# Seven block products for twelve of the pairs in one feed-forward up projection of a two-layer diffusion backbone

## The chip, the core and the metric

The kernel runs on one core of a Trainium2 chip. The metric is the device time of one execution in microseconds (us). Below, TensorE (PE in the rows; PEld is its weight load), VectorE (DVE), ScalarE (ACT), GpSimd (POOL) and the queue of SyncE (SP), which issues nearly all fetches, are the core's engines. SBUF is the core's memory, PSUM the eight banks that TensorE writes to.

## What is computed

Two layers; each is a feed-forward block, a token mixer and a second feed-forward block. There are 256 context tokens and 256 latent tokens of 1024 features; in layer 2, context tokens are only needed until the mixer has read them. The part that matters here:

```python
def modulate(h, shift, scale):
    return h * (1.0 + scale) + shift

def swiglu(u, w_up, w_down):
    a, v = jnp.split(u @ w_up, 2, axis=-1)
    return (jax.nn.silu(a) * v) @ w_down

def ffn_sublayer(h, m, j, w_up, w_down, g, b):
    u = modulate(h, m[:, :, 3 * j], m[:, :, 3 * j + 1])
    return post_norm(h, swiglu(u, w_up, w_down), m[:, :, 3 * j + 2], FFN_RES_W, g, b)
```

The modulation vectors `m` (nine for each layer) are `silu(c) @ w_ada + b_ada`, once for the latent tokens and once for the context. The hidden width is 2816, 22 tiles of 128: a gate tile and a value tile for each, here called a pair.

## The kernel before, in words

All data is kept with features on the partitions, so a block of tokens is 128 features x 512 tokens (`T`; 256 context, then 256 latent, `TL`). Every operand of a large matmul is split into a high and a low part, both in a 32-bit format for TensorE, and a product is three passes: high x high, high x low, low x high (`mm3`, L369 to L375, passes L372 to L374). The low part is the value less the high part.

Weights come in groups: one fetch of 512 KB brings eight blocks of 128x128 in one of three raw buffers (`raw_issue`, L255; tiles `wr`). ScalarE copies the group into its high part (L342, tile `wh`), VectorE subtracts to get the low part (L344, tile `wl`), and the raw buffer goes to the next fetch on SP's queue, in a fixed order (`split_ahead`). Three slots hold split groups; in a down product three more are taken from the activations, which are free by then. A slot is free when TensorE has read its group.

The feed-forward function (`ffn`) begins with the first two pairs, whose matmuls follow the layer norm feature by feature (`k_outer`). Then come the other pairs one by one: eight blocks of the contraction for the gate, eight for the value, 48 matmuls in two banks. `act` applies the SiLU on ScalarE (L760), the product on VectorE (L761) and the split of the hidden tile (L764, L765). Then come the eight row tiles of the down product, 22 blocks each; the last two are done in halves of 256 tokens (`tail`), with all their split weights held for the second half, so in the first half a group is used up in the time of 24 matmuls of 256 columns.

The modulation vectors are made by VectorE on the side: one tile (`ada_part`, L481) is a fetch of 512 KB into a raw buffer of the same three and, for each of the two conditioning vectors, a multiplication with a sum over 1024 elements (L488), then a bias (L492). 128 tiles are spread in program order over the feed-forward blocks: one in each of the up projections' contractions, two in each row of a down product.

The program is written once without a chip, which gives the order of the weight groups, and again to emit. A scheduler sets the order on each engine.

```python
                    if kt == KT // 2:
                        self.ada_part()
...
                if ft in (8, 16):
                    self.ada_part()
```

## Time and profile before

| what | value |
|---|---|
| median of three runs | 2718.85 us (2718.21 to 2720.57) |
| the profiled execution, its own time | 2722.64 us |
| its span, from first to last instruction | 2720.7 us |
| mean granted TensorE clock | 0.991 |
| busy share of the span | PE 98%, DVE 71%, ACT 45%, POOL 13% |
| fetched from memory | 373.63 MB, 139 GB/s over the span |

The profile is of one execution. Busy matmuls overlap in it, since the end of each is modelled: what a matmul costs in a stream is the distance from its start to the next one's start. In a row of the timeline, square brackets give the idle time of the engine before the instruction and what ended it.

The feed-forward stages in this execution: layer 1 first block, pairs to 265 us, down product after it; layer 1 second block, pairs to 1452, down product to 1577; layer 2 first block (the one that is changed), pairs 1604 to 1822, down product to 1945; layer 2 second block (latent tokens alone, so 256 columns), pairs 2511 to 2642.

### The profile page before, as it was taken

The numbers are of one execution on the slowest core, as the hardware profiler recorded it, in microseconds if no ns is written. First come the engines' busy times: TensorE is split into PE (matmuls) and PEld (weight loads), VectorE is DVE, ScalarE is ACT, GpSimd is POOL, SyncE is SP. The second block draws the span as 40 slices with busy tenths as digits, with TensorE's granted clock in tenths as the row PEclk, the third lists the DMA queues.
The fourth block names the chain that finished last, engine by engine and source line by source line (L and its number), as shares of the span: only waits on it lengthen the run. The fifth ranks groups of instructions, "written<-read, shape, count | busy, mean of one in ns | idle before, by whom it ended". The sixth has DMA issues, their size and how long they took to land.

```text
span 2720.7 us, 38673 instructions
## 1 busy us (share of the span) xinstructions
PE 2659.9 (98%) x14869; PEld 2280.2 (84%) x14869; DVE 1928.3 (71%) x3469; ACT 1222.9 (45%) x1755; POOL 353.8 (13%) x296
## 2 busy tenths in 40 slices
PE   9999999999999999999999999999998999999998
PEld 7888897778887888888888888888977898899997
DVE  5788769599877545468887588633697998676654
ACT  4323237963345344433323142332388745574543
POOL 0000132112121000040000130001312112012002
PEclk9999999999999999999999999999999999999999
DMA  7666534134343222235666446532333354343563
GB/s 280 193 189 200 172 122 130 60 99 149 105 134 109 78 86 78 88 99 170 194 195 191 132 129 199 169 120 97 108 123 105 111 174 150 107 142 124 175 191 116
DMA packets 117833, 380.49 MB, mean 140 GB/s; under 512 B 13888, under 2 KB 22352, under 8 KB 117648
## 3 DMA queue, kind: packets, MB, share of 16 engines
q1 hardware_dynamic: 116000, 373.52, 42.5%
q0 software_dynamic: 1504, 4.34, 0.5%
q8 instruction: 116, 1.90, 0.3%
q14 instruction: 69, 0.57, 0.1%
q10 hardware_dynamic: 144, 0.17, 0.0%
HBM read 373.63 MB, written 4.33 MB: 139 GB/s over the span
## 4 chain that ended last, share of the span: by engine, by line
PE 56%; DVE 7%; ACT 3%; issue 2%; DMA 1%; POOL 0%; SPq 0%; POOLq 0%; DVEq 0%; ACTq 0%
PE bank L372 17%; PE bank L373 17%; PE bank L374 17%; PE bank L1282 1%; PE bank L1262 1%; DVE wl L344 1%; DVE x L869 1%; DMA wr<-in_ws_dram 1%; DMA x<-acs_d 1%; DVE f L669 0%; DVE m1l L344 0%; ACT wh L342 0%; PE bank L921 0%; DVE f L670 0%; DVE f L676 0%
## 5 line engine op out<-in xcount | busy, mean ns | idle before, releaser
L342 ACT ACTIVATE wh<-wr 128x1024 fp32r<-128x1024 f32 x388 | 410.2, 1058 | 727.1 <-PE bank L373 493.2
L344 DVE TENSOR_TENSOR wl<-wr,wh 128x1024 fp32r<-128x1024 f32 x388 | 483.6, 1247 | 239.4 <-ACT wh L342 237.6
L488 DVE SCALAR_TENSOR_TENSOR ada_scr<-wr,sb 128x1024 f32<-128x1024 f32 x256 | 316.7, 1237 | 135.9 <-DMA wr<-in_ws_dram 133.2
L372 PE MATMUL bank<-u0h,wh 128*128 128x512 f32 (+1 forms) x660 | 247.1, 376 | 5.5 <-ACT u0h L675 3.8
L372 PE MATMUL bank<-r,wh 128*128 128x512 f32 (+1 forms) x736 | 251.3, 342 | 0.0
L374 PE MATMUL bank<-r,wl 128*128 128x512 f32 (+1 forms) x736 | 249.9, 340 | 0.0
L373 PE MATMUL bank<-r,wh 128*128 128x512 f32 (+1 forms) x736 | 249.7, 340 | 0.0
L374 PE MATMUL bank<-u0h,wl 128*128 128x512 f32 (+1 forms) x660 | 237.2, 360 | 3.9 <-DVE wl L344 3.9
L373 PE MATMUL bank<-u0l,wh 128*128 128x512 f32 (+1 forms) x660 | 236.2, 358 | 2.1 <-DVE u0l L677 2.0
L373 PE MATMUL bank<-u1l,wh 128*128 128x512 f32 (+1 forms) x660 | 235.1, 357 | 0.8 <-DVE u1l L677 0.7
L372 PE MATMUL bank<-u1h,wh 128*128 128x512 f32 (+1 forms) x660 | 233.5, 356 | 0.6 <-ACT u1h L675 0.6
L374 PE MATMUL bank<-u1h,wl 128*128 128x512 f32 (+1 forms) x660 | 234.0, 355 | 0.0
L372 PE MATMUL bank<-u2h,wh 128*128 128x512 f32 (+1 forms) x660 | 233.6, 355 | 0.0
L374 PE MATMUL bank<-u2h,wl 128*128 128x512 f32 (+1 forms) x660 | 233.4, 354 | 0.0
L373 PE MATMUL bank<-u2l,wh 128*128 128x512 f32 (+1 forms) x660 | 233.2, 354 | 0.0
L373 PE MATMUL bank<-u3l,wh 128*128 128x512 f32 (+1 forms) x644 | 228.6, 355 | 1.5 <-DVE u3l L677 1.5
L372 PE MATMUL bank<-u3h,wh 128*128 128x512 f32 (+1 forms) x644 | 228.3, 356 | 0.0
L374 PE MATMUL bank<-u3h,wl 128*128 128x512 f32 (+1 forms) x644 | 228.0, 354 | 0.0
L372 PEld LDWEIGHTS bank<-r,wh 128*128 128x128 f32 x736 | 139.4, 190 | 15.3 <-issue 0.3
L374 PEld LDWEIGHTS bank<-r,wl 128*128 128x128 f32 x736 | 139.5, 190 | 15.1
L373 PEld LDWEIGHTS bank<-r,wh 128*128 128x128 f32 x736 | 139.5, 190 | 14.8
L372 PEld LDWEIGHTS bank<-u0h,wh 128*128 128x128 f32 x660 | 125.6, 191 | 29.7 <-issue 5.6
(530 smaller groups left out, 5919.4 us busy)
## 6 DMA issues: line engine op xcount, KB each, us to landing
wr<-in_ws_dram SPq DMA_DIRECT2D x602, 512.0 KB, 4.0
m1r<-in_ws_dram SPq DMA_DIRECT2D x29, 512.0 KB, 3.9
ada<-in_ws_dram SPq DMA_DIRECT2D x16, 512.0 KB, 9.0
x<-acs_d SPq DMA_DIRECT2D x22, 256.0 KB, 3.4
x<-acs_d SPq DMA_DIRECT2D x39, 128.0 KB, 3.6
x<-in_lw_dram SPq DMA_DIRECT2D x16, 256.0 KB, 3.2
f<-acs_d SPq DMA_DIRECT2D x25, 128.0 KB, 3.4
sb<-s_d SPq DMA_DIRECT2D x6, 512.0 KB, 5.8
```

Source lines behind the costliest of these rows:

```text
L342: self.pin(nc.scalar.activation(hi, raw, AF.Copy))
L344: self.pin(nc.vector.tensor_tensor(lo, raw, hi, op=ALU.subtract))
L372: x = self.pin(nc.tensor.matmul(out, st[0], mv[0], start=start, stop=False, skip_group_check=True))
L373: self.pin(nc.tensor.matmul(out, st[0], mv[1], start=False, stop=False, skip_group_check=True))
L374: self.last_mm = self.pin(nc.tensor.matmul(out, st[1], mv[0], start=False, stop=stop, skip_group_check=True))
L488: nc.vector.scalar_tensor_tensor(self.ada_scr, raw.rearrange("p a b -> p (a b)"), 1.0, self.sb[b], op0=ALU.mult, op1=ALU.mult, accum_out=o ...
L869: nc.vector.scalar_tensor_tensor(ys[:, :, a:z], xs[:, :, a + o:z + o], w(k), ys[:, :, a:z], op0=ALU.mult, op1=ALU.add)
L1262: nc.tensor.matmul(ps[:, 0:256], cc(kt[d], a), vv(a), start=True, stop=True)
L1282: nc.tensor.matmul(cc(po[w], c), lh, rh, start=n == 0, stop=n == len(steps) - 1, skip_group_check=True)
```

## The change

It concerns layer 2's first feed-forward block (`paired`), and the place of the modulation tiles in the others.

Of the 22 pairs there, the first four stay as they were. The other 18 go through `strassen`. Of every three, two are block products and the third is done as before, in four parts. In a block product the weights of a pair are a 2x2 block matrix (gate and value by even and odd blocks of the contraction), the activations are one too (even and odd blocks by context and latent tokens), and the four blocks of the result come from seven products (Winograd's form) of 4 blocks x 3 passes with 256 columns, where eight such products did it before. The sums of weights (four of 128x512 a pair) and of results (three of 128x256) are on VectorE; ScalarE copies what a bank holds between two products that add to the same bank (left half: products 1, 6, 5, 3; the other bank: 7, 4 and 2). Every operand of a product is split by itself, 512 columns at a time, into half a slot (`Part`), so the three slots hold the operands of six products. `products` gives their order.

The differences of the activations are made once, after the layer norm (`columns`): it writes the modulated activations as 32-bit values to a new tile (`ucol`), four subtractions and four splits of 128x1024 follow. For room, that stage has only 8 hidden tiles in split form, the other 14 are kept as they are and split while the first row of the down product runs (`late_parts`, two for each block), the low parts into the activations' place; after that row they are copied out of it on ScalarE (`move`), and the three extra slots of that down product come after it. There are two more raw buffers for the stage.

The modulation tiles leave the stage. A tile is now also taken after 12 blocks of a row in layer 1's first down product, and after 4 and 12 in its second one; what is left goes to layer 2's last up projection. By the order of the built programs the 128 tiles lie so: layer 1 first block 50 before and 56 now, layer 1 second block 52 and 64, layer 2 first block 26 and none, layer 2 second block none and 8.

```diff
+KSPLIT = (0, 2, 4, 6, 1, 3, 5, 7)
+NFULL = 8
+def products(n):
+    r, rest = [], []
+    for p in range(n):
+        last = p == n - 1
+        if p % 3 == 2:
+            r += [(p, 11)] + rest + [(p, 12), (p, 21), (p, 22)]
+            rest = []
+        else:
+            r += [(p, 1), (p, 7)] + rest + [(p, m) for m in ((6, 4, 5, 2) if last else (6, 4, 2, 5))]
+            rest = [(p, 3)]
+    return r + rest
...
+            if m in (1, 7, 11, 21):
+                n = i + 2 * p + (m in (7, 21))
+                R[p, 1 if m in (1, 11) else 7] = self.raw_next(tuple(self.wlist[8 * n:8 * n + 8])), len(self.seq) - 1
+            g = R[p, 1][0]
+            a11, a12 = flat(g[:, 0:4]), flat(g[:, 4:8])
+            if m not in (1, 11, 12):
+                v = R[p, 7][0]
+                a21, a22 = flat(v[:, 0:4]), flat(v[:, 4:8])
+            if m in (1, 11):
+                src = a11
+            elif m == 21:
+                src = a21
+            elif m == 7:
+                R[p, 5] = self.F()
+                sub(R[p, 5], a21, a22, ALU.add)
+                sub(a21, a11, a21)
+                src = a21
+            elif m == 6:
+                sub(a11, R[p, 5], a11)
+                src = a11
+            elif m in (2, 12):
+                src = a12
+            elif m in (4, 22):
+                src = a22
+            else:
+                src = R[p, m]
+            nc.scalar.activation(flat(t.hi), src, AF.Copy)
+            nc.vector.tensor_tensor(flat(t.lo), src, flat(t.hi), op=ALU.subtract)
+            if m == 2:
+                R[p, 3] = self.F()
+                sub(R[p, 3], a12, a11)
+                self.raw_done(R[p, 1][1])
+            elif m == 12:
+                self.raw_done(R[p, 1][1])
+            elif m in (4, 22):
+                self.raw_done(R[p, 7][1])
+            elif m in (3, 5):
+                self.fF(src)
+            self.sparts.append(t)
...
+            if m > 10:
+                out = (x_of if m < 20 else z_of)[p]
+                for b in range(4):
+                    k = 2 * b + m % 10 - 1
+                    self.mm3(out, (t.hi[:, b], t.lo[:, b]), (self.uh[k], self.ul[k]), m % 10 == 1 and b == 0, b == 3)
...
+            X, Z, G, V = x_of[p][:, left], z_of[p], g_of[p], v_of[p]
+            out = Z[:, left] if m in (7, 4) else Z[:, right] if m == 2 else X
+            for b in range(4):
+                if m in (1, 2, 3):
+                    k, s = (2 * b + (m > 1), right if m == 3 else left)
+                    mv = self.uh[k][:, s], self.ul[k][:, s]
+                else:
+                    mv = [x[:, b] for x in self.tparts[{5: 0, 6: 1, 7: 2, 4: 3}[m]]]
+                y = self.mm3(out, (t.hi[:, b], t.lo[:, b]), mv, m in (1, 7) and b == 0, b == 3)
...
+            if m == 1:
+                nc.scalar.activation(G[:, left], X, AF.Copy)
+            elif m == 7:
+                nc.scalar.activation(V[:, right], Z[:, left], AF.Copy)
+            elif m == 6:
+                nc.scalar.activation(V[:, left], X, AF.Copy)
+            elif m == 5:
+                nc.scalar.activation(G[:, right], X, AF.Copy)
+                nc.vector.tensor_tensor(V[:, right], G[:, right], V[:, right], op=ALU.add)
+            elif m == 4:
+                nc.vector.tensor_tensor(V[:, left], Z[:, left], V[:, left], op=ALU.add)
+            elif m == 2:
+                nc.vector.tensor_tensor(G[:, left], Z[:, right], G[:, left], op=ALU.add)
+                nc.scalar.activation(G[:, left], G[:, left], AF.Silu)
+                self.fB(Z)
+            elif m == 3:
+                nc.scalar.activation(G[:, right], X, AF.Silu)
+                self.fB(x_of[p])
+                finish(fts[p], G, V)
+                self.fF(G, V)
...
+        for o, a, b in ((b11, b12, b11), (b12, b22, b12), (b22, b22, b11), (b21, b21, b22)):
+            nc.vector.tensor_tensor(o, a, b, op=ALU.subtract)
+        self.tparts = [[x if self.dry else x.rearrange("p a (b c) -> p (a b) c", c=TL) for x in t] for t in self.tp]
+        for n, src in ((2, b12), (1, b22), (3, b21), (0, b11)):
+            hi, lo = self.tparts[n]
+            nc.scalar.activation(hi, src, AF.Copy)
+            nc.vector.tensor_tensor(lo, src, hi, op=ALU.subtract)
...
+        if paired:
+            self.columns()
+        for ft in range(len(ps) // 2, reg):
             pp = [self.B(), self.B()]
             for i in range(2):
                 for kt in range(KT):
                     w = self.W(("up", l, j, kt, i * NFT + ft))
-                    if kt == KT // 2:
+                    if kt == KT // 2 and not paired:
                         self.ada_part()
                     self.mm3(pp[i][:, c0:], w, (self.uh[kt][:, c0:], self.ul[kt][:, c0:]), kt == 0, kt == KT - 1)
             act(*pp)
...
+            self.strassen(l, j, range(reg, NFT), finish)
+            his = [x[:, i] for t in self.tp for x in t for i in range(2)]
+            spare = [x[:, i] for t in self.up for x in t for i in range(2)]
...
+            for ft in late[:n]:
+                src = pages[ft - NFULL]
+                hi, lo = his.pop(0), spare.pop(0)
+                nc.scalar.activation(hi, src, AF.Copy)
+                nc.vector.tensor_tensor(lo, src, hi, op=ALU.subtract)
...
+            for ft in range(NFULL, NFT):
+                lo = q.tile([P, T], F32R, name=f"hl{l}{jm}_{ft}")
+                nc.scalar.activation(lo, hid[ft][1], AF.Copy)
+                hid[ft] = hid[ft][0], lo
...
                 w = self.W(("down", l, j, ft, m))
-                if ft in (8, 16):
+                if late:
+                    late_parts(2)
+                if not paired and (ft in (8, 12, 16) or ft == 4 and jm):
                     self.ada_part()
                 if m == 1 and ft == 6:
                     self.res_mean(halves)
                 self.mm3(po[:, c0:], w, (hid[ft][0][:, c0:], hid[ft][1][:, c0:]), ft == 0, ft == NFT - 1)
+            if m == 0 and paired:
+                move()
+                more()
             self.res_tile(m, po, halves)
...
+                            n = 2 * (NFULL if self.paired(l, c0) else NFT)
+                            self.rpages = [rp.tile([P, T], F32R, name=f"r{l}{j}_{i}") for i in range(n)]
+                            if self.paired(l, c0):
+                                self.tp = [[rp.tile([P, 2, T], F32R, name=f"t{l}{j}{i}{h}") for h in "hl"]
+                                           for i in range(4)]
+                            else:
+                                self.ada_begin(rp)
```

Three places in VectorE's order. In the names, `wr` and `x10r` are raw buffers, `wh` and `wl` the split slots, `f` work pages, `r` and `hr` hidden tiles, `sb` the conditioning vector. First, a piece of the changed stage. Before, with a modulation tile for each weight group:

```order
L344 TENSOR_TENSOR wl_96<-wr_90,wh_95 128x1024
L488 SCALAR_TENSOR_TENSOR ada_scr,mods_66<-wr_91,sb_10884 128x1024
L488 SCALAR_TENSOR_TENSOR ada_scr,mods_66<-wr_91,sb_10885 128x1024
L492 TENSOR_SCALAR mods_66<-mods_66,par_64 128x2
L488 SCALAR_TENSOR_TENSOR ada_scr,mods_66<-wr_90,sb_10884 128x1024
L761 TENSOR_TENSOR f_110<-bank_117,f_110 128x512
```

Now, a block product's splits (L460), sums of weights (L426) and of results (L546, L548, L544):

```order
L460 TENSOR_TENSOR wl_98<-f_109,wh_97 128x512
L546 TENSOR_TENSOR f_110<-bank_116,f_110 128x256
L460 TENSOR_TENSOR wl_98<-wr_90,wh_97 128x512
L548 TENSOR_TENSOR f_99<-bank_116,f_99 128x256
L460 TENSOR_TENSOR wl_96<-x10r_10946,wh_95 128x512
L460 TENSOR_TENSOR wl_96<-wr_90,wh_95 128x512
L544 TENSOR_TENSOR f_110<-f_99,f_110 128x256
L460 TENSOR_TENSOR wl_94<-f_105,wh_93 128x512
L460 TENSOR_TENSOR wl_94<-x10r_10947,wh_93 128x512
L426 TENSOR_TENSOR f_105<-x10r_10946 128x512
L426 TENSOR_TENSOR x10r_10946<-wr_91,x10r_10946 128x512
L1036 TENSOR_TENSOR hr_5_10945<-f_110,f_99 128x512
```

The tiles are gone from there, and the splits are of half the size and wait for sums. Second, layer 2's last up projection, at the weight groups of the fifth pair (its gate's in the first row, its value's in the last). Before:

```order
L344 TENSOR_TENSOR wl_98<-wr_92,wh_97 128x1024
L761 TENSOR_TENSOR f_100<-bank_117,f_100 128x256
L344 TENSOR_TENSOR wl_96<-wr_90,wh_95 128x1024
L765 TENSOR_TENSOR r_7_18439<-f_100,r_6_18438 128x256
L344 TENSOR_TENSOR wl_94<-wr_91,wh_93 128x1024
```

Now:

```order
L399 TENSOR_TENSOR wl_94<-wr_90,wh_93 128x1024
L996 TENSOR_TENSOR r_5_19157<-f_109,r_4_19156 128x256
L719 SCALAR_TENSOR_TENSOR ada_scr,mods_66<-wr_92,sb_19196 128x1024
L719 SCALAR_TENSOR_TENSOR ada_scr,mods_66<-wr_92,sb_19197 128x1024
L723 TENSOR_SCALAR mods_66<-mods_66,par_64 128x2
L719 SCALAR_TENSOR_TENSOR ada_scr,mods_66<-wr_91,sb_19196 128x1024
L992 TENSOR_TENSOR f_100<-bank_116,f_100 128x256
L719 SCALAR_TENSOR_TENSOR ada_scr,mods_66<-wr_91,sb_19197 128x1024
L996 TENSOR_TENSOR r_7_19159<-f_100,r_6_19158 128x256
L723 TENSOR_SCALAR mods_66<-mods_66,par_64 128x2
L719 SCALAR_TENSOR_TENSOR ada_scr,mods_66<-wr_90,sb_19196 128x1024
L399 TENSOR_TENSOR wl_98<-wr_92,wh_97 128x1024
```

Two and a half modulation tiles (the second to the fourth of eight) stand between the two weight splits of that pair, which had one small operation between them; the first tile stands two splits before this piece, the other four and a half behind it, about one for each split. Third, the middle of layer 1's second down product. Before:

```order
L344 TENSOR_TENSOR wl_96<-wr_92,wh_95 128x1024
L488 SCALAR_TENSOR_TENSOR ada_scr,mods_66<-wr_90,sb_8352 128x1024
L492 TENSOR_SCALAR mods_66<-mods_66,par_64 128x2
L344 TENSOR_TENSOR wl_94<-wr_91,wh_93 128x1024
L560 SCALAR_TENSOR_TENSOR f_112<-bank_123,gp_70,f_112 128x256 x2
```

Now:

```order
L399 TENSOR_TENSOR wl_94<-wr_91,wh_93 128x1024
L719 SCALAR_TENSOR_TENSOR ada_scr,mods_66<-wr_90,sb_8375 128x1024
L719 SCALAR_TENSOR_TENSOR ada_scr,mods_66<-wr_90,sb_8376 128x1024
L723 TENSOR_SCALAR mods_66<-mods_66,par_64 128x2
L719 SCALAR_TENSOR_TENSOR ada_scr,mods_66<-wr_92,sb_8375 128x1024
L719 SCALAR_TENSOR_TENSOR ada_scr,mods_66<-wr_92,sb_8376 128x1024
L723 TENSOR_SCALAR mods_66<-mods_66,par_64 128x2
L719 SCALAR_TENSOR_TENSOR ada_scr,mods_66<-wr_91,sb_8375 128x1024
L791 SCALAR_TENSOR_TENSOR f_101<-bank_120,gp_70,f_101 128x256
L719 SCALAR_TENSOR_TENSOR ada_scr,mods_66<-wr_91,sb_8376 128x1024
L399 TENSOR_TENSOR u2l<-wr_90,u2h 128x1024
```

Three tiles stand between two weight splits there (the thirteenth and fourteenth group after the first), where at most one and a half stood before.

## Rows read from the trace of the kernel before

**Rows 1.** Busy time and share of the span of each engine, whole execution (page, part 1).
```profile
PE 2659.9 (98%) x14869; PEld 2280.2 (84%) x14869; DVE 1928.3 (71%) x3469; ACT 1222.9 (45%) x1755; POOL 353.8 (13%) x296
```

**Rows 2.** Busy time by stretch: from:to, length, then the engines (instructions), clock, DMA.
```profile
core 0: us, PE busy (x) PEld busy (x) DVE busy (x) ACT busy (x) POOL busy (x), PEclk, DMA share, GB/s
265.00:355.00 90.00, 89.65 (x394) 73.58 (x393) 64.43 (x119) 25.61 (x29) 12.96 (x8) 1.00 0.54 171
1452.00:1542.00 90.00, 90.00 (x396) 74.14 (x395) 62.56 (x94) 24.24 (x26) 12.00 (x8) 1.00 0.55 174
1604.00:1822.00 218.00, 218.00 (x963) 180.53 (x962) 142.62 (x213) 67.50 (x86) 0.00 (x0) 1.00 0.50 162
2525.00:2557.00 32.00, 32.00 (x267) 31.89 (x267) 18.80 (x27) 16.87 (x26) 0.00 (x0) 1.00 0.56 181
2510.00:2517.00 7.00, 6.22 (x29) 6.22 (x30) 5.64 (x16) 3.09 (x5) 4.99 (x6) 0.51 0.03 13
```

**Rows 3.** Timeline of ScalarE: start, duration, instruction, idle before; first and last SiLU.
```profile
1631.27 0.58 ACT L760 ACTIVATE f<-bank 128x512 f32<-128x512 f32 x1
...
1816.22 0.58 ACT L760 ACTIVATE f<-bank 128x512 f32<-128x512 f32 x1
...
2540.95 0.37 ACT L760 ACTIVATE f<-bank 128x256 f32<-128x256 f32 x1
...
2638.86 0.37 ACT L760 ACTIVATE f<-bank 128x256 f32<-128x256 f32 x1
```

**Rows 4.** Timeline of VectorE in the changed stage, two places.
```profile
1613.75 1.23 DVE L488 SCALAR_TENSOR_TENSOR ada_scr<-wr,sb 128x1024 f32<-128x1024 f32 x1 [2.69 <-DMA wr<-in_ws_dram]
...
1616.43 1.22 DVE L488 SCALAR_TENSOR_TENSOR ada_scr<-wr,sb 128x1024 f32<-128x1024 f32 x1
...
1639.85 1.22 DVE L344 TENSOR_TENSOR wl<-wr,wh 128x1024 fp32r<-128x1024 f32 x1
1640.98 0.69 DVE L765 TENSOR_TENSOR r<-f,r 128x512 fp32r<-128x512 f32 x1
1641.58 1.22 DVE L488 SCALAR_TENSOR_TENSOR ada_scr<-wr,sb 128x1024 f32<-128x1024 f32 x1
```

**Rows 5.** Timeline of VectorE, ScalarE and TensorE in the last up projection.
```profile
2528.51 0.76 DVE L761 TENSOR_TENSOR f<-bank,f 128x256 f32<-128x256 f32 x2 [3.11 <-PE bank L374]
2529.73 1.22 DVE L344 TENSOR_TENSOR wl<-wr,wh 128x1024 fp32r<-128x1024 f32 x1 [0.46 <-ACT wh L342]
...
2532.68 0.42 DVE L761 TENSOR_TENSOR f<-bank,f 128x256 f32<-128x256 f32 x1
2533.01 1.22 DVE L344 TENSOR_TENSOR wl<-wr,wh 128x1024 fp32r<-128x1024 f32 x1
...
2539.85 0.28 PE L372 MATMUL bank<-u0h,wh 128*128 128x256 f32 x1
2539.98 1.06 ACT L342 ACTIVATE wh<-wr 128x1024 fp32r<-128x1024 f32 x1 [1.51 <-PE bank L373]
2541.07 1.23 DVE L344 TENSOR_TENSOR wl<-wr,wh 128x1024 fp32r<-128x1024 f32 x1 [1.31 <-ACT wh L342]
2542.73 0.28 PE L372 MATMUL bank<-u0h,wh 128*128 128x256 f32 x1
```

**Rows 6.** Issues of weight fetches from 2528 to 2640 us: time to landing.
```profile
DMA to landing us min/median/max: 3.2/4.3/4.5
```

**Rows 7.** Timeline of ScalarE and VectorE about layer 1's second down product.
```profile
1446.89 0.58 ACT L760 ACTIVATE f<-bank 128x512 f32<-128x512 f32 x1
...
1544.74 1.22 DVE L344 TENSOR_TENSOR u3l<-wr,u3h 128x1024 fp32r<-128x1024 f32 x1
```

**Rows 8.** Issues of weight and tile fetches from 1455 to 1545 us: time to landing.
```profile
DMA to landing us min/median/max: 3.2/4.1/5.6
```

**Rows 9.** Timeline of TensorE ahead of layer 2's last up projection.
```profile
2510.78 0.58 PE L372 MATMUL bank<-u0h,wh 128*128 128x256 f32 x1 [3.64 <-ACT u0h L675]
```

More of the change, by code (lines that the diff above doesn't have):

```diff
@@ L105, in __init__, with sections @@
         self.wlist = wlist
+    @staticmethod
+    def sections(wlist):
+        r, last = {}, None
+        for i in range(len(wlist) // 8):
+            w = wlist[8 * i:8 * i + 8]
+            key = w[0][:3] if w[0][0] == "up" and tuple(x[3] for x in w) == KSPLIT else None
+            if key is None or key != last:
+                begin = i
+            if key is not None:
+                r[begin] = (i - begin + 1) // 2
+            last = key
+        return r
     def alloc(self, ctx):
```

158 lines of the change are left out of this document (144 added, 14 removed).

## The prediction, made before the changed kernel was run

> **What bounds the kernel now.** I read the page first, then the table of stages, then single rows. [rows 1] TensorE is busy for 98% of the span. [rows 2] In the stage that the change rewrites (1604 to 1822 us) TensorE is busy for all 218 us, VectorE for 142.6; nothing that VectorE gives up there can shorten it, only fewer or shorter matmuls. In the two stages to which modulation tiles go, the down product of layer 1's second feed-forward (1452 to 1542) and the start of layer 2's last up projection (2525 to 2557), TensorE is also busy throughout, and VectorE is idle for 90.0 - 62.6 = 27.4 and 32.0 - 18.8 = 13.2 us. So there are two questions: what the block products save on TensorE, and whether those idle times hold the tiles.
>
> **TensorE's gain.** [rows 3] The gate's SiLU comes once per pair of projections. From 1631.27 to 1816.22 there are 17 pairs of 48 matmuls with 512 columns: 10.88 us a pair, 226.6 ns a matmul. From 2540.95 to 2638.86, 17 pairs of 48 with 256 columns: 5.76 us, 120.0 ns. So half the columns cost 53%, not 50%. A pair as block products has 7 products x 4 blocks x 3 passes = 84 matmuls of 256 columns: 84 x 0.120 = 10.08 us. The gain is 0.80 us a pair, **9.6 us** for twelve. The six other pairs keep their 48.
>
> **What the block products add.** [rows 4] From start to start, VectorE needs 0.60 us for a 128x512 operation (1640.98 to 1641.58), 1.13 for a weight split of 128x1024 (1639.85 to 1640.98), and [rows 5] 0.33 for one of 256 columns (2532.68 to 2533.01). A block-product pair takes 4 sums and 7 splits of 512 columns, 3 sums of 256, the product with the gate and at most one more split: 13 x 0.60 + 3 x 0.33 = 8.8 of its 10.08 us; a plain pair takes at most 3.6 of 10.88. So VectorE keeps up, and an operand has the five other products in the three slots, 5 x 1.44 = 7.2 us, to be made in. I put this at nothing. Below, it can gain nothing. Above: after a pair that begins alone, TensorE has one product (1.44 us) between filling a bank and adding to it again, in which ScalarE must copy it; six such places at up to 0.7 us are 4 us. The four differences and splits of the activations (8 x 1.13 = 9.0 us) stand on VectorE before the splits of the last two weight groups of the two plain pairs ahead; those two pairs, 21.8 us, cover them, with little left for the first of the two groups: 0 to 2 us. The fourteen late splits (2 x 0.60 each with ScalarE) are hidden behind the first eight down blocks and then run at TensorE's pace; the fourteen copies of low parts run on ScalarE in the next row of products. I put both at nothing; if that cover is gone, the splits cost 14 x 0.60 = 8 us at the most. The 26 tiles that leave this stage hid under TensorE and give back nothing.
>
> **Eight tiles in the last up projection.** [rows 4] A modulation tile takes VectorE 2.68 us from start to start (1613.75 to 1616.43). Eight are 21.4 us. From below: VectorE's 13.2 idle us take that much of it, and splits are early there by [rows 5] 2545.61 - 2542.30 = 3.3 us (a split that starts at 2541.07 and takes 1.23 is for the group after the one that begins at 2542.73, 2.88 us later). 21.4 - 13.2 - 3.3 = 4.9 us of waiting remain even if no fetch is late. From above I walk the order of VectorE's rows as shown, with three fetch buffers and 4.3 us from issue to landing [rows 6]. Tile 1 fits into the 3.11 us idle before 2528.51. Tile 2's buffer is released by the split that ends at 2529.73 + 1.22 = 2530.95, so it lands at 2535.3; VectorE is done with it, and its buffer free, at 2538.2. That buffer takes the next weight group: landed at 2542.5, its high part made by ScalarE in 1.06 us [rows 5], its split over at 2544.8, behind tile 3 and half of tile 4. TensorE wants it at 2539.85 + 0.24 = 2540.1: a wait of 4.7 us. The next groups come out 0.1, 2.5, 2.6, 1.1 and 2.6 us late, since a tile and a split take VectorE and a buffer 4.2 to 4.9 us and TensorE uses a group up in 2.88. Sum 13.6; after the eighth tile it is over. I take **13**, near the walk, as the order on VectorE is fixed and a split can't pass a tile. Bounds: 5 and 17 (fetches of 5 us).
>
> **Twelve more tiles in layer 1's second down product.** They add 12 x 2.68 = 32.2 us to a VectorE idle for 27.4. [rows 7] The down product begins half a pair after 1446.89, at 1452.3; 16.5 groups at 5.44 and 4.5 at 2.88 us later, at 1555.0, TensorE wants the last group, whose split ended at 1544.74 + 1.22 = 1546.0: 9 us early. From below 32.2 - 27.4 - 9.0 is negative: nothing. From above, 17 weight groups and 24 tiles share three buffers: with 4.1 us to landing [rows 8], (17 x (4.1 + 1.06 + 1.22) + 24 x (4.1 + 2.55)) / 3 = 89 us if no buffer ever waits, and VectorE's own work is 17 x 1.13 + 24 x 2.68 + about 9.6 of residuals = 93 us. Two limits this near each other on one in-order engine don't overlap fully: row by row, the last two groups come 7 us late at 4.1 us to landing, and 2 at 3.2. I take **5**, between; bounds 0 and 9. Layer 1's first down product gets six more tiles (16 us) against 25.6 idle: nothing, and at most 2.
>
> **Sum.** -9.6 + 13 + 5 = +8.4 us. The profiled execution took 2722.64 us, so its like would be 2731.0. It lies 3.8 above the median of the runs, 2718.85; on the median the forecast is **2727.2 us**.
>
> **The rivals.** (a) The forecast, with waits in both places: 2724.4 to 2733; chance 0.48.
> (b) Waits at the low ends, from 5 + 0 to 13 + 2: 2714.3 to 2724.2, within 0.2% (5.4 us, about what a measurement can tell from no change). For it: fetches land in 3.2 us at best [rows 8], and VectorE's idle time would do in the second place. Chance 0.30.
> (c) Faster: the tiles are absorbed in the last up projection. This takes one thing: that there the weight splits run at least the 4.9 us further ahead, in VectorE's idle time before 2525, so that the tiles meet filled slots. From 3 us of waiting down it shows as faster: 2709 to 2713. Against it: there are three slots, and each split in [rows 5] starts only after its slot was released. Chance 0.10.
> (d) A clock loss or bank waits on top. [rows 2, 9] TensorE was busy until a wait of 3.64 us before 2510.78, and in 2510 to 2517 the granted clock was 0.51, the lower level of 1.2 GHz; 29 matmuls ran in those 7 us where 58 fit, 3.5 us lost. My first wait is 4.7 us long. Such a fall there and one in the down product cost up to 7, partly hidden, as TensorE waits for VectorE then anyway; with bank waits of 4 or VectorE behind in the block products: 2733 to 2740. Chance 0.12. The Trainium skill, TensorE: Matmul & The Clock Gate, section "Why this matters for your kernels", advises against idle gaps between bursts of matmuls, since the clock then falls; by that rule the first wait alone would add some 3.5 us and the result would be 2730.7.
>
> **How the numbers follow.** Slower by over 0.2% is (a) and (d): 0.60. Within 0.2% is (b): 0.30. Faster is (c): 0.10. The range from 2713 to 2736 takes in (a), (b) and the lower part of (d), and leaves out (c) and the rest of (d), under 2 in 10; the bounds 5 + 0 and 17 + 9 alone give 2714.3 and 2735.3.
>
> **What the next profile would show.** Right: in the stage of block products the SiLU of the twelve pairs comes 10.1 us apart, with TensorE busy throughout; after the start of the last up projection TensorE waits some 4 us for a weight split, then shorter ones five times, all put down to VectorE's L344 row of old, in a stretch of some 30 us; VectorE is over 95% busy there; the last two weight groups of layer 1's second down product are waited for. Wrong: if TensorE doesn't wait in the last up projection, the walk fails and (c) holds; if a block-product pair takes over 10.3 us, the cover there fails, and the term of 9.6 with it.

## The result and the profile after

The changed kernel takes **2746.93 us** (2746.25 to 2748.89, 5 runs) against 2718.85: a ratio of 1.0103, 95% interval 1.0089 to 1.0118, so 28 us slower. The direction of the forecast was right; its size, 2727.2, was short by 20 us, and the result lies outside the range. The profiled execution has a span of 2744.7 us, 24.0 more than the one before, at a granted clock of 0.989.

In the code of the change L399 is the split of a weight group (L344 before), L603 to L605 are the three passes, L719 a modulation tile's product, L991 the SiLU. First the busy times of the whole execution, as [rows 1]:

```profile
PE 2663.7 (97%) x15301; PEld 2298.8 (84%) x15301; DVE 2017.0 (73%) x3633; ACT 1276.0 (46%) x1905; POOL 362.7 (13%) x296
```

That says little. The table of stretches of the changed kernel says where to look, as [rows 2]:

```profile
core 0: us, PE busy (x) PEld busy (x) DVE busy (x) ACT busy (x) POOL busy (x), PEclk, DMA share, GB/s
265.00:355.00 90.00, 87.87 (x387) 72.09 (x386) 78.57 (x143) 24.32 (x28) 12.13 (x8) 1.00 0.60 197
1452.00:1542.00 90.00, 88.61 (x390) 72.72 (x389) 82.56 (x127) 22.25 (x24) 17.86 (x8) 1.00 0.62 201
1542.00:1556.00 14.00, 11.51 (x90) 10.91 (x88) 13.79 (x28) 2.09 (x3) 1.56 (x1) 1.00 0.64 217
1556.00:1571.00 15.00, 10.02 (x55) 8.68 (x56) 8.36 (x12) 2.13 (x3) 4.30 (x4) 0.77 0.49 163
1620.00:1840.00 220.00, 220.00 (x1432) 200.74 (x1431) 157.91 (x252) 113.86 (x222) 1.84 (x1) 1.00 0.30 99
2552.00:2586.00 34.00, 28.14 (x184) 26.68 (x185) 25.72 (x41) 12.24 (x17) 0.00 (x0) 0.85 0.71 212
```

The same for the end of layer 1's second down product in the kernel before:

```profile
1542.00:1556.00 14.00, 14.00 (x115) 13.88 (x114) 5.19 (x10) 2.11 (x3) 3.97 (x4) 1.00 0.38 118
1556.00:1571.00 15.00, 15.00 (x124) 14.89 (x124) 9.12 (x19) 6.67 (x11) 5.45 (x5) 1.00 0.12 37
```

In these 29 us TensorE runs 145 matmuls where it ran 239, and VectorE, which was idle two thirds of the first 14 us, is full. The stage of the block products shows no idle TensorE (220.00 of 220.00); since the ends of matmuls are modelled, that does not rule out short waits, and there are some (see plain below). In the last up projection 184 matmuls run in 34 us, where 283 would fit at 0.12 us each.

I cut the span at rows that both traces have: the SiLU of layer 1's last pair (1446.89 before, 1446.3 after), layer 2's first SiLU (1603.53, 1619.86), the matmuls of the row mean in the second row of that block's down product (1839.7, 1848.6), the first SiLU of layer 2's last up projection (2528.1, 2538.4) and its last one (2638.9, 2663.0).

| stretch | before | after | difference |
|---|---|---|---|
| start to layer 1's last SiLU | 1446.9 | 1446.3 | -0.6 |
| **T**: to layer 2's first SiLU (down product, layer norm, first pairs) | 156.6 | 173.6 | **+17.0** |
| **B**: to the row mean (block products, first down row) | 236.2 | 228.7 | **-7.5** |
| to the last block's first SiLU (rest of the down product, mixer) | 688.4 | 689.8 | +1.4 |
| **L**: first to last SiLU of the last up projection | 110.8 | 124.6 | **+13.8** |
| to the end | 81.9 | 81.8 | -0.1 |

They add up to 24.0, the difference of the spans. A cut at a SiLU is not always a cut at the same matmul: in the changed kernel five matmuls of 512 columns (1.1 us) more stand ahead of layer 2's first SiLU, so 1.1 of T's 17.0 and of B's 7.5 is only moved from one to the other. In T, TensorE's waits in the last rows of the down product of the changed kernel, in brackets with what ended them:

```profile
1553.74 0.28 PE L605 MATMUL bank<-r,wl 128*128 128x256 f32 x1
1556.71 0.58 PE L603 MATMUL bank<-r,u2h 128*128 128x256 f32 x1 [2.69 <-ACT u2h L397]
1557.09 0.41 PE L604 MATMUL bank<-r,u2h 128*128 128x256 f32 x1
1560.02 0.58 PE L605 MATMUL bank<-r,u2l 128*128 128x256 f32 x1 [2.51 <-DVE u2l L399]
```

and what VectorE and GpSimd did meanwhile:

```profile
1555.60 2.17 DVE L719 SCALAR_TENSOR_TENSOR ada_scr<-wr,sb 128x1024 f32<-128x1024 f32 x1
1557.69 2.27 DVE L399 TENSOR_TENSOR u2l<-wr,u2h 128x1024 fp32r<-128x1024 f32 x1
...
1554.43 2.24 POOL L828 TENSOR_TENSOR f<-f,f 128x512 f32<-128x512 f32 x1 [13.44 <-DVE mods L723]
1556.64 2.24 POOL L830 TENSOR_TENSOR f<-f,f 128x512 f32<-128x512 f32 x1
```

A modulation product and the split that TensorE waits for stand in line on VectorE, and both take 2.2 us instead of 1.22. GpSimd's two sums, which had waited 13.4 us for VectorE's queue, run just then, and take 2.24 us each where the same sums take 1.29 in the kernel before (at 1546.89 and 1548.14). The Trainium skill, Trainium Architecture — The Big Picture, section "What this means for kernel authors", says that VectorE and GpSimd hold their shared memory port by an exclusive lock; these durations agree, though no run here took GpSimd's sums away. After the two waits the granted clock is 0.77 in the stretch, so part of it at the lower level of 1.2 GHz: matmuls start 0.22 us apart (1560.40, 1560.62, 1560.83) where 0.12 is the pace.

### The profile page after: what moved, and what is told of

It reads as the page before. It is cut to its first block, busy times and chain, and to the rows that moved or that the text cites. A ratio compares the mean times of both kernels' runs of the same rounds, so it can differ in the third digit from the quotient of the medians.

```text
span 2744.7 us, 39966 instructions
## 1 busy us (share of the span) xinstructions
PE 2663.7 (97%) x15301; PEld 2298.8 (84%) x15301; DVE 2017.0 (73%) x3633; ACT 1276.0 (46%) x1905; POOL 362.7 (13%) x296
## 4 chain that ended last, share of the span: by engine, by line
PE 71%; DVE 14%; ACT 6%; DMA 4%; issue 3%; POOL 1%; DVEq 0%; SPq 0%; POOLq 0%; ACTq 0%
PE bank L603 22%; PE bank L604 22%; PE bank L605 22%; DMA wr<-in_ws_dram 3%; DVE wl L399 2%; DVE ada_scr L719 2%; DVE x L1162 1%; PE bank L1575 1%; ACT wh L397 1%; PE bank L1555 1%; DMA x<-acs_d 1%; ACT x L1215 1%; PE bank L1214 1%; DVE f L900 1%; PE bank L1392 1%
## 5 line engine op out<-in xcount | busy, mean ns | idle before, releaser
L397 ACT ACTIVATE wh<-wr 128x1024 fp32r<-128x1024 f32 x351 | 370.8, 1057 | 641.7 <-PE bank L604 412.3
L399 DVE TENSOR_TENSOR wl<-wr,wh 128x1024 fp32r<-128x1024 f32 x351 | 439.4, 1253 | 205.2 <-ACT wh L397 202.3
L719 DVE SCALAR_TENSOR_TENSOR ada_scr<-wr,sb 128x1024 f32<-128x1024 f32 x256 | 319.6, 1248 | 73.4 <-DMA wr<-in_ws_dram 70.8
L603 PE MATMUL bank<-u0h,wh 128*128 128x512 f32 (+1 forms) x648 | 239.6, 372 | 8.6 <-ACT wh L397 4.1
L605 PE MATMUL bank<-u0h,wl 128*128 128x512 f32 (+1 forms) x648 | 229.3, 354 | 8.1 <-DVE wl L399 8.1
L603 PE MATMUL bank<-r,wh 128*128 128x512 f32 (+1 forms) x678 | 232.2, 343 | 0.0
L605 PE MATMUL bank<-r,wl 128*128 128x512 f32 (+1 forms) x678 | 230.3, 340 | 0.5 <-DVE wl L399 0.5
L604 PE MATMUL bank<-r,wh 128*128 128x512 f32 (+1 forms) x678 | 230.1, 340 | 0.0
L603 PE MATMUL bank<-u2h,wh 128*128 128x512 f32 (+1 forms) x648 | 226.1, 350 | 0.8 <-ACT u2h L906 0.8
L603 PE MATMUL bank<-u1h,wh 128*128 128x512 f32 (+1 forms) x648 | 225.4, 350 | 0.6 <-ACT u1h L906 0.6
L605 PE MATMUL bank<-u2h,wl 128*128 128x512 f32 (+1 forms) x648 | 225.8, 349 | 0.0
L605 PE MATMUL bank<-u1h,wl 128*128 128x512 f32 (+1 forms) x648 | 225.6, 349 | 0.0
L603 PE MATMUL bank<-u3h,wh 128*128 128x512 f32 (+1 forms) x632 | 220.1, 351 | 0.3 <-ACT u3h L906 0.3
L605 PE MATMUL bank<-u3h,wl 128*128 128x512 f32 (+1 forms) x632 | 220.0, 349 | 0.0
L826 POOL TENSOR_TENSOR f<-f,f 128x512 f32<-128x512 f32 (+1 forms) x6 | 8.4, 1398 | 1094.1 <-DVE f L791 1094.1
L603 PEld LDWEIGHTS bank<-u0h,wh 128*128 128x128 f32 x648 | 123.4, 191 | 33.0 <-ACT wh L397 6.7
L605 PEld LDWEIGHTS bank<-u0h,wl 128*128 128x128 f32 x648 | 124.1, 192 | 27.4 <-DVE wl L399 11.1
L604 PEld LDWEIGHTS bank<-u0l,wh 128*128 128x128 f32 x650 | 124.8, 192 | 21.3 <-issue 5.2
```

Of the source, the lines that this page charges most:

```text
L397: self.pin(nc.scalar.activation(hi, raw, AF.Copy))
L399: self.pin(nc.vector.tensor_tensor(lo, raw, hi, op=ALU.subtract))
L603: x = self.pin(nc.tensor.matmul(out, st[0], mv[0], start=start, stop=False, skip_group_check=True))
L604: self.pin(nc.tensor.matmul(out, st[0], mv[1], start=False, stop=False, skip_group_check=True))
L605: self.last_mm = self.pin(nc.tensor.matmul(out, st[1], mv[0], start=False, stop=stop, skip_group_check=True))
L719: nc.vector.scalar_tensor_tensor(self.ada_scr, raw.rearrange("p a b -> p (a b)"), 1.0, self.sb[b], op0=ALU.mult, op1=ALU.mult, accum_out=o ...
```

## The experiments

Each run was set against the kernel before on the same chip (medians there 2719.2 to 2720.9), so I compare ratios; 0.001 is 2.7 us. T, B and L are the stretches of the table above, from each run's own trace, one execution each; where the program is the same, T differs by up to 1.7 us between runs (the change, spread8, no8), L by up to 2.3.

| run | ratio (95%) | T | B | L |
|---|---|---|---|---|
| before | 1 | 156.6 | 236.2 | 110.8 |
| **the change** | 1.0103 (1.0089 to 1.0118) | 173.6 | 228.7 | 124.6 |
| no12 | 1.0047 (1.0035 to 1.0060) | 161.1 | 229.0 | 125.0 |
| no6 | 1.0058 (1.0046 to 1.0071) | 162.9 | 228.7 | 124.8 |
| vec12 | 1.0079 (1.0065 to 1.0093) | 169.1 | 228.7 | 124.3 |
| fetch12 | 1.0068 (1.0055 to 1.0080) | 167.8 | 229.0 | 122.7 |
| no8 | 1.0053 (1.0039 to 1.0067) | 175.3 | 229.0 | 110.8 |
| spread8 | 1.0073 (1.0061 to 1.0086) | 174.5 | 228.7 | 114.8 |
| tiles | 1.0094 (1.0080 to 1.0107) | 167.9 | 236.2 | 124.0 |
| plain | 1.0120 (1.0106 to 1.0133) | 174.0 | 235.0 | 123.1 |
| nosub | 1.0062 (1.0048 to 1.0076) | 161.0 | 229.3 | 124.1 |
| ring | 1.0045 (1.0033 to 1.0058) | 159.8 | 228.2 | 124.3 |
| afteru | 1.0116 (1.0100 to 1.0131) | 170.6 | 236.3 | 123.9 |
| early20 | 1.0129 (1.0116 to 1.0143) | 183.0 | 228.8 | 110.8 |
| early20u | 1.0138 (1.0124 to 1.0152) | 180.8 | 235.9 | 110.8 |
| mix | 1.0073 (1.0060 to 1.0085) | 160.3 | 235.8 | 113.5 |

### Which part costs what: no12, no8, tiles, plain

**no12** and **no8** leave tiles out:

```diff
+                if l == 0 and jm and ft in (4, 12):
+                    self.ada_leave()
-                if not paired and (ft in (8, 12, 16) or ft == 4 and jm):
+                elif not paired and (ft in (8, 12, 16) or ft == 4 and jm):
...
+                    if kt == KT // 2 and l == DEPTH - 1 and jm:
+                        self.ada_leave()
```

> The changed kernel with the twelve added modulation tiles of layer 1's second down product left out (neither fetched nor multiplied; their columns are set to zero), all else as in the change. Theory A, the tiles: they lost 15 us there (11 in the last columns of the product, 4 in the layer norm and first pairs of layer 2 behind it), so the time falls from 2746.9 to about 2732 (2729 to 2736), and the first half's sums of the layer norm end near 1561 in the trace again. Rival B, the preparation of the block products: the f32 copies of the columns and the subtractions of `columns` stand on VectorE in the same stretch and cause it; then the time stays over 2741. If only the 4 us in the layer norm are B's, it is about 2736.

> The changed kernel with the eight modulation tiles of layer 2's last up projection left out (columns set to zero). Theory A: they cost 13.8 us in the profile, so the time is about 2733 (2731 to 2736) and the waits of TensorE between 2550 and 2585 are gone. Rival C: those waits belong to the weights' transfers at the start of the stage and only changed their name; then it stays over 2741.

Both fell as theory A had it: 0.0056 x 2719 = 15.2 us and 0.0050 x 2719 = 13.6 us. In no8, L is back at 110.8. In no12, T fell by 12.5 and 4.5 remain, so theory B holds for a part. Rival C falls.

**tiles** has the tiles moved and no block products; **plain** keeps all of the change but for the seven products:

```diff
-                    if kt == KT // 2:
+                    if kt == KT // 2 and not (c0 == 0 and l == DEPTH - 1):
...
-                if ft in (8, 16):
+                if not (c0 == 0 and l == DEPTH - 1) and (ft in (8, 12, 16) or ft == 4 and jm):
```

```diff
-        if p % 3 == 2:
+        if n:
```

> The kernel before with the modulation tiles alone moved as in the change (none in layer 2's first block, the same tiles more in layer 1's two down products, eight in layer 2's last up projection), without block products. Theory A: 2718.9 + 15 + 14 = about 2748 (2743 to 2752), as slow as the change itself or slower. The forecast's own terms, 5 and 13, would give 2737. Rival B: without the f32 columns only the 14 remain, 2733.

> The changed kernel with all 18 pairs of the stage as eight products each in four parts (no seven-product pair), so that the same parts, pools and tiles are kept. Theory A: the twelve block pairs gave 6.3 us (0.53 each) in the trace, so this is about 2753 (2751 to 2756). By the forecast's 0.80 each it is 2756.5. If the block products give nothing, 2747.

tiles: T +11.3, L +13.2, ratio 1.0094: moving the tiles alone makes the kernel 25.6 us slower, with no block product in it. plain: B is 235.0 against the change's 228.7, so twelve block pairs give **6.3 us**, 0.53 each and not 0.80; the ratios differ by 0.0017, 4.6 us, with intervals that overlap, so the 6.3 rest on the stretch. The start of a threesome of pairs on TensorE, in the changed kernel, shows the same:

```profile
1640.01 0.28 PE L603 MATMUL bank<-u0h,wh 128*128 128x256 f32 x1
...
1646.24 0.28 PE L604 MATMUL bank<-t100l,wh 128*128 128x256 f32 x1
1646.52 0.39 PE L603 MATMUL bank<-u0h,wh 128*128 128x256 f32 x1
1646.74 0.28 PE L604 MATMUL bank<-u0l,wh 128*128 128x256 f32 x1
...
1671.65 0.28 PE L603 MATMUL bank<-u0h,wh 128*128 128x256 f32 x1
```

The next threesome begins 31.64 us later. Three pairs took 32.64 [rows 3], so two block pairs save 1.00. Within the products the pace is the 0.120 that I had taken, but in the whole stage 26 matmuls start 0.10 to 0.15 us later than that, as at 1646.52 and 1646.74: 3.2 us in all, which is what is missing from 9.6. The operand changes at every product and most changes cost nothing. The rows of the weight loads and of VectorE name the cause:

```profile
1646.51 0.19 PEld L603 LDWEIGHTS bank<-u0h,wh 128*128 128x128 f32 x1 [0.19 <-DVE f L546]
...
1656.20 0.19 PEld L603 LDWEIGHTS bank<-t100h,wh 128*128 128x128 f32 x1 [0.16 <-ACT f L541]
...
1646.04 0.42 DVE L546 TENSOR_TENSOR f<-bank,f 128x256 f32<-128x256 f32 x1 [0.21 <-PE bank L605]
```

L546 is VectorE's sum that reads the half bank which product 4 has just filled; product 2 comes next in the program and goes to the other half of that bank. L541 is ScalarE's copy of what product 6 left in the bank that product 5 adds to. TensorE's weight load waits ten times for the first and twice for the second in the stage, up to 0.2 us each, and after each wait the next matmul is late too; the other two late starts follow a weight load that was idle for 0.04 us. plain has no such wait. No run changed the order of the products.

### Why twelve tiles cost 12.5 us: vec12, fetch12, no6

vec12 multiplies values that lie in the chip; fetch12 fetches and reads two columns:

```diff
+    def ada_vec(self):
...
+                nc.vector.scalar_tensor_tensor(self.ada_scr, self.sb[1 - b], 1.0, self.sb[b],
+                                               op0=ALU.mult, op1=ALU.mult, accum_out=o[:, b:b + 1])
...
+    def ada_fetch(self):
...
+            raw = self.raw_next((("adb", l, j, k),))
+            self.nc.vector.tensor_scalar(self.mods[l][:, j, k, :], raw.rearrange("p a b -> p (a b)")[:, 0:2], 0.0,
+                                         None, op0=ALU.mult)
+            self.raw_done()
```

> The changed kernel in which the twelve added tiles of layer 1's second down product are multiplied on VectorE as before, but from values that are in the chip already: no fetch and no raw buffer (those columns then hold other values). Without the twelve the time was 15 us over... the kernel before less 15 against the change. Theory V, VectorE's queue: the 12 x 2.5 us of products ahead of the weight groups' low halves cost the 11 us by themselves, so the time stays within 4 us of the change, at a ratio of 1.009 to 1.011 to the kernel before. Theory F, fetches and the three raw buffers: it falls to that of the run without the twelve, 1.0047 (1.004 to 1.006).

> The reverse: the twelve tiles are fetched into the raw buffers in their turn, but of each only two columns are read, by one VectorE instruction of some 0.2 us (the products are left out). Theory V: as without the twelve, ratio 1.0047 (1.004 to 1.006). Theory F: within 4 us of the change, 1.009 to 1.011. If both this and the last run lie between, the cost comes of a buffer that is held until VectorE gets to its tile, which needs both.

Neither theory alone: over no12's 161.1, T is 8.0 longer with the products and 6.7 with the fetches. Busy times of layer 1's second down product, first without the twelve, then vec12, then fetch12:

```profile
1452.00:1542.00 90.00, 90.00 (x401) 74.38 (x400) 62.03 (x95) 23.67 (x26) 12.02 (x8) 1.00 0.54 172
1542.00:1571.00 29.00, 29.00 (x236) 28.57 (x234) 13.69 (x25) 9.54 (x16) 11.22 (x11) 1.00 0.26 83
```

```profile
1452.00:1542.00 90.00, 89.28 (x399) 73.56 (x397) 87.53 (x137) 22.64 (x24) 17.70 (x8) 1.00 0.51 164
1542.00:1571.00 29.00, 24.36 (x179) 23.65 (x178) 15.70 (x33) 4.93 (x9) 4.31 (x5) 0.88 0.23 73
```

```profile
1452.00:1542.00 90.00, 90.00 (x401) 74.37 (x400) 60.04 (x99) 23.19 (x25) 13.33 (x8) 1.00 0.68 224
1542.00:1571.00 29.00, 25.15 (x181) 24.43 (x180) 12.64 (x26) 5.89 (x10) 4.46 (x6) 0.88 0.31 113
```

With the products alone VectorE is busy for 87.5 of 90 us at an easy 164 GB/s. With the fetches alone it is busy for 60 and the core moves 224 GB/s through three buffers. Both ratios lie between the theories, for which the second expectation had a third reading, a cost that needs products and fetches together; but each costs 6.7 to 8.0 us by itself. What TensorE waits for is another thing than in the change. In the last 29 us no weight group is late for it in either run; it waits once, for the sums of the layer norm (L875). One row of vec12, then three of fetch12:

```profile
1557.59 0.80 PE L875 MATMUL bank<-f,ones 128*128 128x256 f32 x1 [4.63 <-POOL f L849]
```

```profile
1557.18 0.79 PE L875 MATMUL bank<-f,ones 128*128 128x256 f32 x1 [3.85 <-POOL f L849]
1553.97 1.26 POOL L849 TENSOR_TENSOR f<-f,f 128x512 f32<-128x512 f32 x1 [11.70 <-DVE f L812]
1551.81 1.23 DVE L399 TENSOR_TENSOR u3l<-wr,u3h 128x1024 fp32r<-128x1024 f32 x1 [1.14 <-ACT u3h L397]
```

GpSimd's sums wait for VectorE's residual rows (L812), and these stand behind the last weight split, which ends near 1553 in both runs and at 1545.0 without the twelve. So in vec12 VectorE's work makes its queue late, and in fetch12 its waits do: up to 1553 it waits 20.8 us for the high parts of weight groups, 3.3 without the twelve; the stretch behind has a mean clock of 0.88 in both.

**no6** leaves out the six at hidden tile 4 (`if l == 0 and jm and ft == 4: self.ada_leave()`).

> The changed kernel with six of the twelve added tiles of layer 1's second down product left out (those at hidden tile 4; three tiles a column stay, where the kernel before had two and the change has four). Theory L, a price for each tile: half of the cost goes, ratio 1.0075 (1.007 to 1.008). Theory S, slack: three a column fit into the room that is there and the fourth is what comes late; then as without the twelve, 1.0047 to 1.0055. Against S: what remained with only products or only fetches of all twelve was about half as well.

T is 162.9: six cost 1.8 us and the other six 10.7. The ratio, 1.0058, is just above theory S's range and far from L's. Theory S, and its rows:

```profile
1452.00:1542.00 90.00, 88.47 (x389) 72.63 (x388) 75.73 (x118) 24.16 (x26) 12.14 (x8) 1.00 0.65 198
1542.00:1571.00 29.00, 29.00 (x234) 28.60 (x233) 16.71 (x31) 8.27 (x15) 9.00 (x9) 1.00 0.34 108
```

With three tiles a row TensorE waits for nothing at the end, and for 1.53 us at the row mean at 1471.29, which is most of the 1.8; the six fill VectorE's idle time, which had room for them. The run took out the six at hidden tile 4 and left those at 12; that the number counts and not the place was not tried the other way round.

### Eight tiles in the last up projection: spread8

```diff
-                    if kt == KT // 2 and not paired:
+                    if kt == KT // 2 and not paired and (not l or i == 0 and ft % 2 == 0):
```

> The change with the eight tiles of layer 2's last up projection spread: one in every second pair (5.76 us each) in place of two in each of the first four. Theory S: between them VectorE has 2.6 us of 5.76 free in a pair and a tile wants 2.5, so most of the 13.8 us goes, ratio 1.005 to 1.007. Theory L: the same 1.7 us for each, ratio 1.010.

L is 114.8: 4.0 us for the eight tiles that cost 13.8 when they stood together. How close they stand sets the price; the ratio, 1.0073, is just above theory S's range. Three of the eight waits in the change:

```profile
2552.39 0.39 PE L603 MATMUL bank<-u0h,wh 128*128 128x256 f32 x1 [2.08 <-ACT wh L397]
2553.65 0.58 PE L605 MATMUL bank<-u0h,wl 128*128 128x256 f32 x1 [0.76 <-DVE wl L399]
...
2567.60 0.39 PE L605 MATMUL bank<-u0h,wl 128*128 128x256 f32 x1 [0.98 <-DVE wl L399]
```

### The 4.5 us that are left in T: nosub, ring, afteru

Without the twelve, T's 4.5 us lie between the second half's layer norm sums and layer 2's first SiLU (36.0 us against 31.5). Rows of VectorE in that run, L913 the write of the modulated activations to `ucol` (L907 in the change), L399 a weight split:

```profile
1569.61 1.59 DVE L399 TENSOR_TENSOR wl<-wr,wh 128x1024 fp32r<-128x1024 f32 x1 [0.63 <-ACT wh L397]
1576.16 0.48 DVE L797 SCALAR_TENSOR_TENSOR f<-bank,gp,f 128x256 f32<-128x256 f32 x1 [4.96 <-PE bank L605]
1576.56 0.40 DVE L913 TENSOR_SCALAR uc<-f,gp,gp 128x256 f32<-128x256 f32 x1
```

and of the kernel before (L677 the low part behind that write):

```profile
1566.72 0.95 DVE L677 TENSOR_TENSOR u0l<-f,u0h 128x256 fp32r<-128x256 f32 x2
...
1573.71 0.62 DVE L677 TENSOR_TENSOR u2l<-f,u2h 128x256 fp32r<-128x256 f32 x1
```

Before, the first half's rows were done while TensorE still worked at the down product. Now they stand behind a row that waits for its end, and VectorE idles 4.96 us. The explanation to be tested: `ucol` is laid over memory of the stage before, so its writes must wait for that stage's last readers. ring and afteru give the first half a page of the ring as before; afteru copies it later (the second piece below), ring leaves that copy out; nosub leaves out the subtractions.

```diff
-        up = self.F(keep=True) if nxt and not self.with_u else None
+        up = self.F(keep=True) if nxt and not (self.with_u and i) else None
...
+                if self.with_u and not i:
+                    nc.scalar.activation(self.ucol[:, q, k % 2, s], u, AF.Copy)
```

> The run without the twelve tiles, and also without the four subtractions that `columns` makes of the f32 columns (left out; the high and low parts are then of the columns themselves). That run lost 4.5 us between the second half's sums of the layer norm and layer 2's first SiLU against the kernel before (36.2 us against 31.7). Theory Q: the subtractions among the rows cause it, so it falls to 32 us, ratio 1.003. Theory P: the rows of the first half that wait for the pool's memory cause it; then it stays at 35 to 36 us, ratio 1.004 to 1.005.

> The run without the twelve tiles, with the first half's layer norm rows written to the ring's pages as in the kernel before and not copied into the f32 columns at all (the copies are left out; `columns` takes the second half for both). Theory P: 32 to 34 us in that stretch, ratio 1.003 to 1.004, and nothing given back behind it, so that what the copying version lost between the first SiLU and the first down column (236.3 us against 228.7) is its copies. Theory Q: 36 us, ratio 1.0047.

> The change with the first half's layer norm rows written to the ring's pages and copied later, as in the last run of the call before, whose trace had 2.3 us of the 4.5 back between the second half's sums and layer 2's first SiLU (33.7 us against 36.0, and 31.7 in the kernel before). Theory P: the same here, ratio 1.009 to 1.010, and 33 to 35 us there. If VectorE's backlog of the twelve tiles hides it, no change.

By this cut nosub has 34.6 us, ring 34.7 and afteru 33.7, but both of its ends move between the runs. A surer count takes the matmuls in T at their pace (0.2267 us for 512 columns, 0.12 for 256) and calls the rest of T lost: 4.9 us before, 8.2 in no12, 8.8 in nosub, 5.8 in ring, 20.7 in the change, 17.9 in afteru. So of the 4.5 us 1.1 are the five matmuls ahead of the SiLU and 3.3 are lost. nosub gave nothing back: Q falls. ring gave back 2.4 and afteru 2.8, so P accounts for most of the 3.3; the 0.9 that remain in ring stay open. The ratios alone would not show it: nosub's 1.0062 is above both theories, ring's 1.0045 is near Q's.

afteru lost more than it gained: B is 236.3 against 228.7, and ring, without the copies, has 228.2, so the copies cost that. In afteru's trace TensorE waits 1.71, 0.22 and 1.76 us at 1621 to 1625 for weight splits that stand behind the work of `columns` on ScalarE and VectorE, at a mean clock of 0.83 (1615 to 1635). afteru's ratio, 1.0116, is no better than the change's.

### Looking for a better place: early20, early20u, mix

early20 takes the twenty tiles to a third place in layer 1's up projections, early20u adds afteru's edit, mix joins no6's density, spread8, afteru's edit and six tiles in the first up projection.

```diff
+                    if kt == i == 0 and l == 0 and (ft % 2 == 0 or ft == 21):
+                        self.ada_part()
```

> The change with its twenty late tiles put elsewhere: a third tile in every second pair of layer 1's two up projections, the second down product as in the kernel before, none in layer 2's last up projection. If the ledger of the traces holds, what is left of the change is 4.5 us more in the layer norm before layer 2 (seen without the twelve tiles too), -7.4 in the stage of the block products and +1.5 in its first down column: -1.4 us, so 2717 to 2722 with up to 4 for the third tiles. If the third tiles are late as well, 2726 or more.

> The same, and the first half of the layer norm's rows is written to a page of the ring, as in the kernel before, and copied by ScalarE into the f32 columns later. Theory P: the 4.5 us come from those rows' having to wait until the pool of the columns, which lies where layer 1's hidden tiles were, comes free after the last product that reads them (no VectorE row of them before 1576 in the trace without the twelve); then this takes 3 to 5 us off the last run, 2713 to 2718. Theory Q: they come from the subtractions of `columns` among the rows of the second half; then nothing changes, or it gets slower by ScalarE's eight copies.

> Block products with the tiles put where the runs leave room: three a column in both down products of layer 1, one more in every third pair of layer 1's first up projection (six), the eight of layer 2's last up projection in every second pair, and the early layer norm rows. Theory S: the kernel before less 3.7 (2.2 - 7.4 + 1.5) and up to 8 for tiles that still come late: 2715 to 2724. Theory L, 1.0 to 1.7 us for each added tile: 2735 to 2745.

early20 came out in the second branch of its expectation, above 2726; early20u missed; mix landed in theory L's range, though not by a price for each tile. A third tile in every second pair of an up projection is late too: from the first to the last SiLU the first block takes 211.8 us in early20 (204.2 before) and the second 221.0 (211.8), and more of the lag shows up behind the stage. TensorE in early20, at the row mean of layer 1's first down product, which waits for VectorE's residual rows:

```profile
289.21 0.39 PE L604 MATMUL bank<-r,u3h 128*128 128x512 f32 x1
298.50 2.07 PE L803 MATMUL bank<-f,ones 128*128 128x512 f32 x2 [8.90 <-DVE f L791]
```

mix placed the tiles better (T 160.3, L 113.5), but its six in the first up projection brought that row mean 8.3 us late (292.4 against 284.1), and its copies took B's gain. No version beat the kernel before. By the table, as an estimate, block products without any cost of tiles would be worth 4.5 - 7.5 + 1.4 = -1.6 us, less than a measurement can tell.

## Why the prediction was wrong in size

- **Eight tiles in the last up projection, 13**: measured 13.8, by L and by no8. The walk gave the sum but not its parts: eight waits of 8.9 us in all (each start less the start before and the pace of 0.12), not 13.6, the longest 2.2 and not 4.7; the other 4.9 are matmuls at the lower clock (0.85 in the mean of that stretch), which the walk did not hold; that the sum fitted is luck. Rival (c) fell.
- **Twelve more tiles in layer 1's second down product, 5, bounds 0 and 9**: this step failed most. They cost 12.5 us (T, change less no12). The row-by-row walk had the right waits ("the last two groups come 7 us late"; 2.69 + 2.51 and smaller ones, 8.6 in six waits counted in the same way), and I halved it against a lower bound that credited splits with 9 us of lead. The runs show that products alone and fetches alone each make VectorE's queue some 8 us late: the text's own 32.2 us of work against 27.4 idle is vec12. And a split was not the only thing that could be late: in those two runs it was the layer norm's sums behind VectorE's residual rows, which the walk did not follow. The upper bound also lacked what follows a wait: 3.3 us of matmuls at the lower clock (0.77 in the stretch), and the split that took 2.27 us beside GpSimd.
- **What the block products add, 0**: 3.3 of lost time in T, 1.6 behind the row mean and the 3.2 of the next item. For T I costed the subtractions of `columns` (nosub: nothing, right), and not that `ucol`'s writes wait for memory of the stage before (ring, afteru: 2.4 to 2.8). From the row mean to the layer norm's sums TensorE takes 102.03 us before and in tiles, and 103.6 in all fourteen traces with the changed stage, plain among them. In the change that is one weight group that comes late, at 1858.69, and its copy on ScalarE had waited 4.37 us for TensorE to free a slot. That the three extra slots come later in this stage fits it; no run gave them earlier.
- **TensorE's gain, 9.6**: 6.3 by plain, and a block pair takes (31.64 - 10.88) / 2 = 10.38 us. The price of 84 matmuls was right: outside the late starts the pace is 0.1198 us. What failed is the cover that I put at nothing, with 4 us as its bound: the waits for a bank cost 3.2. I saw ScalarE's copy as the danger, and most waits are for VectorE's sum, between two products that follow each other into the halves of one bank. My sign for it, 10.3 us a pair, came true, though TensorE's row shows no idle time.
- **Six more tiles in the first down product, 0 to 2**: 1.8 us, and not nothing. From the last SiLU of the pairs to the start of the down product's last matmul it is 129.8 us before and 131.6 now (130.6 to 134.6 in the other runs with just these six added there). The -0.6 of the table hides it: in this execution the pairs ended 1.3 us earlier, and the way to the second block was 1.1 shorter.
- **The rivals**: (d) named the clock fall and waits for banks, and was nearest; both are in the runs. Matmuls at the lower clock cost 4.9 us in the last up projection and 3.3 at the end of T, against its "up to 7", and the bank waits 3.2 against its 4. Its range ended at 2740, since the down product's own waits and T's lost time were in no rival. The rule cited there (the Trainium skill, TensorE: Matmul & The Clock Gate, "Why this matters for your kernels") agrees in kind in two places, 0.77 and 0.85 after waits.

Sum of the misses on the profile: 7.5 for the twelve, 3.3 + 1.6 in T and behind the row mean, 3.3 of TensorE's gain and 0.8 for the eight make 16.5, against the 15.6 between the forecast's +8.4 and the span's +24.0. The 0.9 too many are -0.6 at the start, -0.1 at the end and the scatter of the stretch behind the row mean.

## What to carry to other kernels

Work put "beside" a busy engine is free only up to the idle time of every resource on its way, and then it costs at once: three tiles a row cost 1.8 us, the fourth 10.7. Add demand and capacity per stretch for each resource; where two are near their limit, take the walk's late end and add the clock behind the wait. Before you take work out of a stage, ask whether its new home has the room that the old one had. And do not take a busy row of TensorE for the absence of waits: measure from start to start, and read the rows of its weight loads.

## What was not expected of the hardware

With three 512 KB buffers, fetches alone made VectorE's queue late at 224 GB/s (fetch12), while 198 GB/s (no6) delayed nothing at the end of the stage; whether buffers or transfers set that was not tried. A VectorE operation of 128x1024 took 2.2 us in place of 1.22 beside GpSimd's sums, and these 2.24 in place of 1.29. Waits of 0.16 to 0.2 us for a bank, 3.2 us in a stage, stood in the rows of the weight loads while TensorE's own row showed 220.00 busy of 220.00.
